# Unused tiles shift three operands of the matmuls against the weight tiles by multiples of 64 bytes

## The chip, the cores and the metric

The kernel runs on one core of a Trainium2 chip. The metric is the device time of one execution in microseconds (us); lower is better. TensorE (PE in the profile) multiplies, and a separate instruction loads its stationary operand (PEld). VectorE is DVE, ScalarE is ACT, GpSimd is POOL, SyncE is SP.

## What is computed

Two transformer blocks run one after the other on 256 tokens of width 2048, in float32. The first has four mixers (pooling, spatial gating, sliding-window attention, convolution), the second a state-space and an attention group, and then an expert layer with 16384 experts. Nearly all of the arithmetic is in products with large weight matrices:

```python
h = jnp.einsum('bsd,de->bse', x, w_in[l])                       # 2048 x 18688
merged = merged + gates[:, :, i] * jnp.einsum('bsc,cd->bsd', branches[i], w_branch[l, i])
out = jnp.einsum('bsd,de->bse', merged, w_out[l])
...
proj = h @ w_in                                                 # second block
x = x + jnp.concatenate([y_ssd, y_fox], axis=-1) @ w_out
q = (t @ wq)                                                    # expert layer: keys
act = jax.nn.gelu(jnp.einsum('thkd,td->thk', u[ib], tb))        # 16384 experts, u and v
return jnp.einsum('thk,thkd->td', gb * act, v[ib])
```

The kernel multiplies the tokens with all rows of `u` and all of `v`, and weights the results with a matrix that is zero for experts that were not chosen.

## The kernel before

**Weights come as a stream of chunks.** Each chunk is 128 partitions by 2048 float32. SyncE loads it into a tile `wr`; then `split` cuts it into halves of 1024 and makes two tiles of each: ScalarE rounds it to `wh` (float32r), and VectorE writes the rest, `wr - wh`, to `wl`. The activations are held in the same two parts: `XH` and `XL` (128 x 16 x 256), `YH` and `YL` (128 x 8 x 256) for the outputs of the four mixers, and `whh` and `whl` for the last product.

**Each product is three matmuls**: high by high, low by high, high by low. Four forms carry nearly all of the matmuls:

- `T_chunk`: 128 weight columns are stationary (`wh`, `wh`, `wl`), and 256 columns of `XH`, `XL`, `XH` move. All of `w_in`, most of the second block, `wq` and `u` go this way.
- `wb_chunk`: the same with `YH`, `YL`, `YH` moving, for `w_branch`.
- `N_chunk`: turned round, 128 columns of `XH`, `XL`, `XH` are stationary and 512 columns of `wh`, `wh`, `wl` move (`w_out`, and parts of both input products).
- `V_chunk`: as `N_chunk`, with `whh`, `whl`, `whh` stationary, for `v` (the last 700 us).

In a profile's row `pm<-XL,wh` the first name behind the arrow moves and the second is stationary; `pm` and `bg` are tiles of PSUM. Every matmul has a weight load of its own.

**Between the chunks**, background tasks (`bg()`, which calls `tasks.tick`) issue the small matmuls of the mixers and of the expert choice; the rows name them `bg<-...`. The order of all of them is made when the program is built, from a table of costs.

**Where tiles lie.** A pool lays its tiles one behind the other in a partition, in the order in which the code asks for them. The pool `per` has `XH`, `XL`, `X0`, `X1`, constants and small tiles; behind it come the pools of `wr`, `wh` and `wl`, then `a1` with `B4`, `gap`, `YH`, `YL`, `R`, `CV`, `GC`, `VQ` and small ones. `gap` is padding, of which 16 columns are used (`sk`). A block of `XH` or `YH` that moves is 1024 bytes long, and a stationary block of weights 512 bytes, and every block begins at a multiple of its length from its tile's start. So the distance of any moving block to any stationary block, modulo 512 bytes, is that of the tiles' starts.

Of the kernel before, what the change touches and what calls it, by code (L numbers as in the profile page):

```python
# [6 lines left out]
F32 = mybir.dt.float32  # L7
# [8 lines left out]
P = 128  # L16
# [181 lines left out]
def kern(tc, A, out):  # L198
    nc = tc.nc
    with ExitStack() as ctx:  # L200
        ctx.enter_context(tc.manual_schedule())
        _kern(tc, nc, ctx, A, out)


def _kern(tc, nc, ctx, A, out):
    tasks = Tasks(4)
    V, SC, G, PE = Meter(nc.vector, tasks, "dve"), Meter(nc.scalar, tasks, "act"), nc.gpsimd, Meter(nc.tensor, tasks, "pe")
    per = ctx.enter_context(tc.tile_pool(name="per", bufs=1))
# [4 lines left out]
    dram = ctx.enter_context(tc.tile_pool(name="dram", bufs=1, space=DRAM))  # L213

    XH = per.tile([P, KT, S], FR, name="XH")
    XL = per.tile([P, KT, S], FR, name="XL")
    X = [per.tile([P, D], F32, name=f"X{t}") for t in range(2)]
    cst = per.tile([P, 7, P], F32, name="cst")
    par = per.tile([P, N_PAR], F32, name="par")
# [13 lines left out]
    def pv(name, i=0, n=1):  # L233
        o, _ = PAR[name]
        return par[:, o + i:o + i + n]

    def row_ap(name):
        o, w = ROW[name]
        src = A["rows"]
        return bass.AP(tensor=src.tensor, offset=src.offset + o, ap=[[0, P], [1, w]])  # L240
# [51 lines left out]
    def T_chunk(evac):  # L292
        def fn(half, hi, lo):
# [5 lines left out]
            for kk in range(8):  # L299
                k = half * 8 + kk  # L300
                PE.matmul(o, h[:, kk], XH[:, k], start=k == 0, stop=False)
                PE.matmul(o, h[:, kk], XL[:, k], start=False, stop=False)
                PE.matmul(o, l[:, kk], XH[:, k], start=False, stop=k == KT - 1)
                if kk == 2:
# [5 lines left out]
    def N_chunk(kq, evac, korder=(0, 1, 2, 3), hold=False, lead=None):  # L310
        def fn(half, hi, lo):
# [6 lines left out]
            def part(t, kq, half, h, l):  # L318
                ts = slice(t * P, (t + 1) * P)
                for kk in range(2):  # L320
                    k = korder[kq] * 4 + half * 2 + kk
                    first = kq == 0 and half == 0 and kk == 0
                    last = kq == 3 and half == 1 and kk == 1
                    PE.matmul(ps[t], XH[:, k, ts], h[:, kk], start=first, stop=False)
                    PE.matmul(ps[t], XL[:, k, ts], h[:, kk], start=False, stop=False)
                    PE.matmul(ps[t], XH[:, k, ts], l[:, kk], start=False, stop=last)
                    if t == 0 and kk == 0:
# [44 lines left out]
    a1 = p1.enter_context(tc.tile_pool(name="a1", bufs=1))  # L372
    w1 = p1.enter_context(tc.tile_pool(name="w1", bufs=2))

    B4 = [a1.tile([P, 1024], F32, name=f"B4{i}") for i in range(4)]
    gap = a1.tile([P, 176], F32, name="gap")
    YH = a1.tile([P, 8, S], FR, name="YH")
    YL = a1.tile([P, 8, S], FR, name="YL")
    R = a1.tile([P, 8 * 286 + 8 * 272], F32, name="R")
    AP_ = R[:, :8 * 272].rearrange("p (j t) -> p j t", j=8)  # L380
# [6 lines left out]
    Q = VQ.rearrange("p (j t) -> p j t", j=8)  # L387
    U_ = X[0].rearrange("p (j t) -> p j t", j=8)
    GA = X[1].rearrange("p (j t) -> p j t", j=8)
    kT = a1.tile([P, S], F32, name="kT")  # L390
# [15 lines left out]
    def start_split():  # L406
        for g in range(4):
            SC.copy(XH[:, g * 4:(g + 1) * 4], xq[g])
            V.tensor_sub(XL[:, g * 4:(g + 1) * 4], xq[g], XH[:, g * 4:(g + 1) * 4].bitcast(F32))
            if g < 2:  # L410
# [87 lines left out]
    def conv_gen(ln):  # L498
# [13 lines left out]
        for stat in range(2):  # L512
# [4 lines left out]
            m = w1.tile([P, S], F32, name="cm")  # L517
            V.tensor_reduce(m, (sq if stat else CV).rearrange("p j t -> p t j"), axis=AX.X, op=OP.add)
            yield WAIT
# [102 lines left out]
    def attn_gen(u):  # L622
        def make(ln):
# [24 lines left out]
            m2 = sm[:, 0, :nq].rearrange("p (v j) -> p v j", v=2)  # L648
            V.tensor_reduce(sm[:, 0, :nq], L3, axis=AX.X, op=OP.max)
            V.tensor_tensor(m2, m2, sks, op=OP.max)  # L650
# [58 lines left out]
    def split_Y(src):  # L709
        for g in range(4):  # L710
            s = slice(2 * g, 2 * g + 2)
            SC.copy(YH[:, s], src[:, s])
            V.tensor_sub(YL[:, s], src[:, s], YH[:, s].bitcast(F32))

# [9 lines left out]
    def wb_chunk(br, jj):  # L724
        def fn(half, hi, lo):
# [3 lines left out]
            for k in range(8):  # L729
                PE.matmul(o, h[:, k], YH[:, k], start=k == 0, stop=False)  # L730
                PE.matmul(o, h[:, k], YL[:, k], start=False, stop=False)
                PE.matmul(o, l[:, k], YH[:, k], start=False, stop=k == 7)
                if k == 2:
# [21 lines left out]
    for br, (_, need, ysrc) in enumerate(order):  # L755
# [4 lines left out]
        for jj in range(8):  # L760
            def pre_y(need=need, ysrc=ysrc, br=br):
# [5 lines left out]
                if br == 2:  # L767
                    nc.gpsimd.dma_start(X[0], A["xN"][0])
                    nc.gpsimd.dma_start(X[1], A["xN"][1])
                    nc.gpsimd.dma_start(GC.rearrange("p j t -> p (j t)"), row_ap("ln_g"))  # L770
# [16 lines left out]
    def split_M(a, b):  # L787
        for g in range(a, b, 2):
            s = slice(g, g + 2)
            SC.copy(XH[:, s], M[:, s])  # L790
            V.tensor_sub(XL[:, s], M[:, s], XH[:, s].bitcast(F32))

# [28 lines left out]
    def to_T(t, lnw, hooks={}):  # L821
        for k0 in range(0, KT, 2):
# [6 lines left out]
            for k in (k0, k0 + 1):  # L829
                V.scalar_tensor_tensor(XL[:, k, t * P:(t + 1) * P], p[:, k - k0], pv(lnw, k),  # L830
                                       hs[:, k - k0].bitcast(F32), op0=OP.mult, op1=OP.subtract)
# [430 lines left out]
    def split_y(g0, g1):  # L1262
        YS, YF = b2["YS"], b2["YF"]
        for g in range(g0, g1, 2):
            s = slice(g, g + 2)
            y = YS[:, s] if g < 8 else YF[:, g - 8:g - 6]
            SC.copy(XH[:, s], y)
            V.tensor_sub(XL[:, s], y, XH[:, s].bitcast(F32))

# [498 lines left out]
```

## Time and profile before

| | |
|---|---|
| median of 3 runs | 3110.59 us (3110.5 to 3112.77) |
| the profiled execution | 3108.64 us, of it 3106.9 us from the first to the last instruction (the span) |
| PE busy | 3062.3 us, 99% of the span, 22026 matmuls |
| PE weight loads busy | 2858.2 us, 92% |
| DVE, ACT, POOL busy | 71%, 51%, 7% |
| granted TensorE clock | 0.995 of full speed over the span |

Matmuls are pipelined: one is shown for 276 to 281 ns, but in a row of them the next begins after a little over 113 ns. Busy time of PE therefore says only that there is always a matmul in flight. The number to read is the distance from one start to the next, the spacing. It comes from the start times of a timeline, or from a stretch's length divided by its count of matmuls; such a count includes those that reach over the stretch's edges, about two.

### The profile page before, as it was taken

The numbers are of one execution on the slowest core, as the hardware profiler recorded it, in microseconds if no ns is written. First come the engines' busy times: TensorE is split into PE (matmuls) and PEld (weight loads), VectorE is DVE, ScalarE is ACT, GpSimd is POOL, SyncE is SP. The second block draws the span as 40 slices with busy tenths as digits, with TensorE's granted clock in tenths as the row PEclk, the third lists the DMA queues.
The fourth block names the chain that finished last, engine by engine and source line by source line (L and its number), as shares of the span: only waits on it lengthen the run. The fifth ranks groups of instructions, "written<-read, shape, count | busy, mean of one in ns | idle before, by whom it ended". The sixth has DMA issues, their size and how long they took to land.

```text
span 3106.9 us, 53221 instructions
## 1 busy us (share of the span) xinstructions
PE 3062.3 (99%) x22026; PEld 2858.2 (92%) x22026; DVE 2200.2 (71%) x3173; ACT 1577.5 (51%) x2205; POOL 223.8 (7%) x187
## 2 busy tenths in 40 slices
PE   8999999999999989999999999999999999999998
PEld 8899999999999869897799999999999888888887
DVE  8899865555555567655579989788796666666665
ACT  4444565444444445555444457667675444444444
POOL 0000000000000020100000003232240000000000
PEclk9999999999999989999999999999999999999999
DMA  7555555555555535433545665766758766666664
GB/s 275 182 200 199 182 182 188 203 182 199 190 202 182 188 121 190 149 135 138 190 150 178 230 214 189 263 235 227 269 195 323 284 234 228 255 244 246 240 218 149
DMA packets 92226, 640.62 MB, mean 206 GB/s; under 512 B 10272, under 2 KB 10448, under 8 KB 17744
## 3 DMA queue, kind: packets, MB, share of 16 engines
q1 hardware_dynamic: 78192, 559.06, 50.2%
q0 software_dynamic: 13504, 77.63, 6.9%
q8 instruction: 173, 2.83, 0.4%
q14 instruction: 69, 0.57, 0.1%
q10 hardware_dynamic: 288, 0.52, 0.0%
HBM read 601.53 MB, written 35.65 MB: 205 GB/s over the span
## 4 chain that ended last, share of the span: by engine, by line
PE 97%; ACT 1%; DVE 1%; issue 1%; DMA 0%; SPq 0%; DVEq 0%; ACTq 0%
PE pm L194 92%; PE bg L194 4%; ACT wh L194 0%; DMA wr<-w_in 0%; DVE wl L194 0%; DVE X L194 0%; DVE XL L194 0%; ACT XH L194 0%; ACT KZ L194 0%; ACT L194 0%; SPq L398 0%; ACT PX L194 0%; ACT XS L194 0%; DVE PX L194 0%; DVE keys L194 0%
## 5 line engine op out<-in xcount | busy, mean ns | idle before, releaser
L194 DVE TENSOR_TENSOR wl<-wr,wh 128x1024 fp32r<-128x1024 f32 x1050 | 1291.3, 1233 | 833.6 <-ACT wh L194 824.3
L194 ACT CAST wh<-wr 128x1024 fp32r<-128x1024 f32 x1054 | 1109.0, 1053 | 1383.1 <-PE pm L194 1330.1
L194 PE MATMUL pm<-XH,wh 128*128 128x256 f32 x4976 | 1393.6, 280 | 8.0 <-ACT wh L194 8.0
L194 PE MATMUL pm<-XH,wl 128*128 128x256 f32 x4976 | 1383.3, 278 | 1.1 <-DVE wl L194 1.1
L194 PE MATMUL pm<-XL,wh 128*128 128x256 f32 x4976 | 1383.0, 278 | 0.0
L194 PEld LDWEIGHTS pm<-XH,wh 128*128 128x128 f32 x4976 | 940.5, 189 | 12.8 <-ACT wh L194 8.0
L194 PEld LDWEIGHTS pm<-XL,wh 128*128 128x128 f32 x4976 | 937.1, 188 | 1.8 <-issue 1.4
L194 PEld LDWEIGHTS pm<-XH,wl 128*128 128x128 f32 x4976 | 935.1, 188 | 1.6 <-DVE wl L194 1.6
L194 PE MATMUL pm<-wh,whl 128*128 128x512 f32 x1024 | 398.3, 389 | 0.0
L194 PE MATMUL pm<-wh,whh 128*128 128x512 f32 x1024 | 398.3, 389 | 0.0
L194 PE MATMUL pm<-wl,whh 128*128 128x512 f32 x1024 | 398.3, 389 | 0.0
L194 PEld LDWEIGHTS pm<-wh,whh 128*128 128x128 f32 x1024 | 192.2, 188 | 39.9
L194 PEld LDWEIGHTS pm<-wh,whl 128*128 128x128 f32 x1024 | 192.2, 188 | 39.9
L194 PEld LDWEIGHTS pm<-wl,whh 128*128 128x128 f32 x1024 | 192.2, 188 | 39.9
L194 PE MATMUL pm<-wh,XH 128*128 128x512 f32 x448 | 178.8, 399 | 1.8 <-ACT XH L194 1.8
L194 PE MATMUL pm<-wh,XL 128*128 128x512 f32 x448 | 176.9, 395 | 1.9 <-DVE XL L194 1.9
L194 PE MATMUL pm<-wl,XH 128*128 128x512 f32 x448 | 177.0, 395 | 0.0
L1453 POOL TENSOR_TENSOR keys<-cst,t 128x512 f32<-128x512 f32 x64 | 136.5, 2132 | 209.6 <-ACT ga L194 209.4
L194 PE MATMUL pm<-YH,wh 128*128 128x256 f32 x512 | 144.1, 281 | 0.0
L194 PE MATMUL pm<-YL,wh 128*128 128x256 f32 x512 | 143.7, 281 | 0.0
L194 PE MATMUL pm<-YH,wl 128*128 128x256 f32 x512 | 143.7, 281 | 0.0
L194 DVE SCALAR_TENSOR_TENSOR CV<-R,par,CV 128x256 f32<-128x256 f32 x240 | 116.8, 487 | 7.3
(276 smaller groups left out, 2381.8 us busy)
## 6 DMA issues: line engine op xcount, KB each, us to landing
wr<-w_in SPq DMA_DIRECT2D x190, 1024.0 KB, 4.8
wr<-uT SPq DMA_DIRECT2D x128, 1024.0 KB, 4.9
wr<-v SPq DMA_DIRECT2D x128, 1024.0 KB, 4.9
wr<-w_branch SPq DMA_DIRECT2D x32, 1024.0 KB, 4.8
wr<-w_out SPq DMA_DIRECT2D x32, 1024.0 KB, 4.8
wr<-wq SPq DMA_DIRECT2D x16, 1024.0 KB, 4.8
Ad<-ast POOLq DMA_DIRECT2D x16, 1024.0 KB, 5.1
Gd<-stg POOLq DMA_DIRECT2D x16, 1024.0 KB, 11.5
```

The source lines that it names most:

```text
L194: return f(out, *a, **k)
L1453: G.tensor_tensor(x, it, t3[:, 0, n0:n0 + 4, None].to_broadcast([P, 4, P]), op=OP.subtract)
```

## The change

Three tiles that nothing reads or writes are added, and `gap` is made 128 bytes shorter:

```diff
     XH = per.tile([P, KT, S], FR, name="XH")
+    per.tile([P, 16], F32, name="gaph")
     XL = per.tile([P, KT, S], FR, name="XL")
+    per.tile([P, 112], F32, name="gapx")
...
-    gap = a1.tile([P, 176], F32, name="gap")
+    gap = a1.tile([P, 144], F32, name="gap")
     YH = a1.tile([P, 8, S], FR, name="YH")
+    a1.tile([P, 16], F32, name="gapy")
     YL = a1.tile([P, 8, S], FR, name="YL")
```

`gaph` is 64 bytes and `gapx` 448, together 512; so all that lies behind them in `per`, and the weight tiles, keep their place modulo 512. On every engine the built program has the same instructions in the same order with the same waits as before. What differs is addresses:

| start in the partition, modulo 512 | before | after |
|---|---|---|
| `XH` | 128 | 128 |
| `XL` | 128 | 192 |
| `YH` | 128 | 0 |
| `YL` | 128 | 64 |
| `wh`, `wl` (all buffers), `whh`, `whl` | 448 | 448 |
| `R`; `CV`, `GC`, `VQ` | 128; 64 | 64; 0 |
| `ga`, `gb` (expert choice) | 0 | 0 |

The distance, start of the moving tile minus start of the stationary tile modulo 512, becomes:

| moving, stationary | matmuls | before | after |
|---|---|---|---|
| `XH`, `wh` and `XH`, `wl` | 2 x 4976 | 192 | 192 |
| `XL`, `wh` | 4976 | 192 | 256 |
| `YH`, `wh` and `YH`, `wl` | 2 x 512 | 192 | 64 |
| `YL`, `wh` | 512 | 192 | 128 |
| `wh`, `XH` and `wl`, `XH` | 2 x 448 | 320 | 320 |
| `wh`, `XL` | 448 | 320 | 256 |
| `wh` or `wl`, `whh` or `whl` | 3 x 1024 | 0 | 0 |
| `gb`, `ga` | 256 | 0 | 0 |

## Rows read from the trace of the kernel before

**Rows 1.** The page: busy by engine, granted clock in 40 slices, the chain.

```profile
PE 3062.3 (99%) x22026; PEld 2858.2 (92%) x22026; DVE 2200.2 (71%) x3173; ACT 1577.5 (51%) x2205; POOL 223.8 (7%) x187
...
PEclk9999999999999989999999999999999999999999
...
PE 97%; ACT 1%; DVE 1%; issue 1%; DMA 0%; SPq 0%; DVEq 0%; ACTq 0%
PE pm L194 92%; PE bg L194 4%; ACT wh L194 0%; DMA wr<-w_in 0%; DVE wl L194 0%; DVE X L194 0%; DVE XL L194 0%; ACT XH L194 0%; ACT KZ L194 0%; ACT L194 0%; SPq L398 0%; ACT PX L194 0%; ACT XS L194 0%; DVE PX L194 0%; DVE keys L194 0%
```

**Rows 2.** The page's groups, one per form: count | busy us, mean ns | idle before.

```profile
L194 PE MATMUL pm<-XL,wh 128*128 128x256 f32 x4976 | 1383.0, 278 | 0.0
...
L194 PE MATMUL pm<-wh,whl 128*128 128x512 f32 x1024 | 398.3, 389 | 0.0
...
L194 PE MATMUL pm<-wh,XL 128*128 128x512 f32 x448 | 176.9, 395 | 1.9 <-DVE XL L194 1.9
...
L194 PE MATMUL pm<-YL,wh 128*128 128x256 f32 x512 | 143.7, 281 | 0.0
```

**Rows 3.** Timeline of PE, two stretches of T_chunk: start us, us, what.

```profile
195.04 0.28 PE L194 MATMUL pm<-XH,wh 128*128 128x256 f32 x1
195.16 0.28 PE L194 MATMUL pm<-XL,wh 128*128 128x256 f32 x1
...
196.10 0.28 PE L194 MATMUL pm<-XH,wh 128*128 128x256 f32 x1
...
204.15 0.28 PE L194 MATMUL pm<-XH,wh 128*128 128x256 f32 x1
...
205.17 0.28 PE L194 MATMUL pm<-XH,wh 128*128 128x256 f32 x1
```

**Rows 4.** Timeline of the weight loads beside the second stretch.

```profile
204.15 0.19 PEld L194 LDWEIGHTS pm<-XL,wh 128*128 128x128 f32 x1
204.26 0.19 PEld L194 LDWEIGHTS pm<-XH,wl 128*128 128x128 f32 x1
```

**Rows 5.** Timeline of PE: background matmuls between two stretches.

```profile
198.81 0.28 PE L194 MATMUL pm<-XH,wl 128*128 128x256 f32 x1
198.93 0.60 PE L194 MATMUL bg<-B,VQ 128*128 128x128 f32 x4
199.29 0.37 PE L194 MATMUL pm<-XH,wh 128*128 128x256 f32 x1
...
510.86 0.66 PE L194 MATMUL bg<-B,vN 128*64 128x128 f32 x8
511.45 0.38 PE L194 MATMUL pm<-XH,wh 128*128 128x256 f32 x1
```

**Rows 6.** Windows, PE: stretch, busy (matmuls), granted clock, DMA share, GB/s.

```profile
514.00:1038.00 524.00, 524.00 (x4451) 1.00 0.54 192
1040.00:1126.00 86.00, 86.00 (x370) 1.00 0.53 184
1675.00:1855.00 180.00, 179.85 (x1587) 1.00 0.61 216
```

**Rows 7.** Windows of the tile XL, then of YL: the matmuls that read it.

```profile
190.00:513.00 323.00, 219.39 (x789) 1.00 0.54 189
514.00:1038.00 524.00, 287.74 (x1024) 1.00 0.54 192
1675.00:2402.00 727.00, 562.11 (x2036) 1.00 0.65 236
...
514.00:1038.00 524.00, 128.99 (x460) 1.00 0.54 192
```

**Rows 8.** Timeline of PE, first and last of long rows: N_chunk, then V_chunk.

```profile
100.14 0.39 PE L194 MATMUL pm<-wh,XH 128*128 128x512 f32 x1
...
141.34 0.39 PE L194 MATMUL pm<-wh,XH 128*128 128x512 f32 x1
...
2500.08 0.39 PE L194 MATMUL pm<-wh,whl 128*128 128x512 f32 x1
...
2539.97 0.39 PE L194 MATMUL pm<-wh,whh 128*128 128x512 f32 x1
```

**Rows 9.** Timeline of PE: a background group of the expert choice.

```profile
1858.56 0.28 PE L194 MATMUL pm<-XH,wl 128*128 128x256 f32 x1
1858.67 0.63 PE L194 MATMUL bg<-gb,ga 128*128 128x256 f32 x4
1859.15 0.28 PE L194 MATMUL pm<-XH,wh 128*128 128x256 f32 x1
1859.26 0.28 PE L194 MATMUL pm<-XL,wh 128*128 128x256 f32 x1
...
1860.17 0.28 PE L194 MATMUL pm<-XH,wh 128*128 128x256 f32 x1
```

## The prediction

> **What bounds the kernel now.** I read the page first: its chain of work lies on PE for 97% of the span, nearly all of it in the matmuls that write `pm`, and the granted clock stands at 0.9 or more of its upper level, 2.4 GHz, in 39 of 40 slices [rows 1]. Data, splits and evictions are hidden: in the groups the idle time ahead of the matmuls is 0.0 to 1.9 us over hundreds or thousands of them [rows 2]. So the time is the sum of the spacings of some 22,000 matmuls, and a change of addresses can only count through a spacing. No instruction, wait or transfer is added, removed or moved.
>
> The second view is the timeline of PE, and there one form, T_chunk, has two paces. From 195.04 to 196.10 us nine spacings take 1.06 us, 117.8 ns each; from 204.15 to 205.17 us nine take 1.02 us, 113.3 ns each [rows 3]. Operands, shapes and distances are the same, nothing waits, and the clock is the full one. I call them the wide and the tight pace; they differ by 4.4 ns a matmul. A pace holds until other matmuls come between: the group at 198.93 us stands between the wide stretch and the tight one, and the group at 510.86 us begins a wide stretch [rows 5] that then lasts, since no further group comes: 524 us from 514 us on hold 4451 matmuls, two of them over the edges, 117.8 ns each; N_chunk behind it keeps on, 86 us for 370, 233.5 ns. The expert layer has the tight one instead: 180 us for 1587, some 113.5 ns with its few small gaps [rows 6].
>
> So something that is neither a wait nor the clock lengthens the spacing. The weight load of the next matmul begins when the current one begins: `XH`, `wh` moves from 204.15 us on, and the load for `XL`, `wh` behind it starts at the same 204.15 us [rows 3, 4]. My reading, which the trace suggests and does not prove, is that the moving stream and the next weight load meet in SBUF, and that their relative place decides how often one holds the other up; the pace would come from the phase between the two, and the distance of the addresses would be the other half of the same sum.
>
> One pair of rows speaks of the distance alone. N_chunk and V_chunk have the same shape, 512 moving columns to one load; V_chunk runs at distance 0 and N_chunk at 320. In N_chunk, entered from a tight stretch, 180 spacings from 100.14 to 141.34 us take 41.20 us, 228.9 ns each; in V_chunk 176 spacings from 2500.08 to 2539.97 us take 39.89 us, 226.7 ns each [rows 8]. That is 2.2 ns a matmul between two distances.
>
> **The change part by part.** The sum is made against the profiled execution, 3108.64 us, which lies 1.95 us under the median of the three runs.
>
> *XL against wh in T_chunk, 192 to 256, 4976 matmuls [rows 2].* The trace has no row for 256 at this width. Bounds: at best XL loses what the wide pace costs it. Of the XL matmuls 1023 lie in the long wide stretch, and of the 788 from 190 to 513 us, where the groups of rows 5 alternate the paces, I take half (an estimate); with as rough a 200 in the other mixed places that is some 1600 [rows 7], so 1600 x 4.4 ns = -7 us. At worst 256 behaves as the worst that I see at 256 columns: in the expert choice `gb` moves over `ga` at distance 0, and six spacings around such a group, from 1858.56 to 1859.26 us, take 0.70 us, 116.7 ns each, 3.3 more than the tight 113.3 (the starts are rounded to 10 ns, so up to 4.5) [rows 9]; 4976 x 4.5 ns = +22 us. In between stands the pair of rows 8: if 256 is to 192 as 320 is to 0, it costs 2.2 ns, 4976 x 2.2 ns = +11 us. I take that, because 256 lies halfway between 192, whose tight pace is the least of any form here (half of V_chunk's 226.7 is also 113.3), and 320, which is the longer of the two in rows 8.
>
> *YH and YL, 192 to 64 and 128, 512 of each of three matmuls [rows 2].* 459 of the 512 triples lie in the long wide stretch [rows 7], where they pay 3 x 4.4 = 13.3 ns, 6 us together. Bounds: at best all of that vanishes, -6 us; at worst the 4.5 ns of rows 9 come on top of the wide pace that they have now, 1536 x 4.5 ns = +7 us. Neither 64 nor 128 has a row of its own, so I take 0.
>
> *XL as stationary in N_chunk, 320 to 256, 448 matmuls [rows 2].* Treating 256 as like 320, as above, this is 0; as like V_chunk's distance it is 448 x -2.2 ns = -1 us.
>
> *`R`, `CV`, `GC`, `VQ` and small tiles move by 64 bytes.* VectorE and ScalarE work on them, with 29% and 49% of the span free [rows 1]; nil, and a longer operation there would lie under PE's stream.
>
> *Which pace each stretch gets.* Taken as now.
>
> Sum: +11 us, 3108.6 to 3120, and as a median 3122 us, 0.4% slower.
>
> A rule speaks against any effect. The Trainium skill, "SBUF — State Buffer", "Who interferes with whom", says that TensorE has two independent read ports, one for the moving operand and one for the weight load, and that it never waits on anyone; "TensorE: Matmul & The Clock Gate", "Step-by-step: what each phase is for", says that loading the next weights takes no read bandwidth from the running matmul. By that rule the sum is 0 and the time 3111 us. The two paces of rows 3 at one clock, without a wait, do not agree with it, nor do the two of rows 8.
>
> **The rivals.**
>
> *The wide pace goes (faster).* The long wide stretch hangs on one group at 510.86 us. If the new distances shift the phase so that this group leaves the tight pace behind it, 4449 matmuls gain 4.4 ns, 19.8 us, and the 368 of N_chunk behind them 233.5 - 228.9 = 4.6 ns, 1.7 us. With XL at 0 to 2.2 ns the whole is -21 to -10 us: 3089 to 3100, say 3095 us. For it: the groups flip the pace between neighbouring stretches [rows 5], so which one a stretch gets hangs on a little shift. Against: the flips follow from the groups, which stay. It decides from the first stretch in which a different pace stands at the same matmul.
>
> *Nothing moves.* Distances of whole 64-byte steps might be alike as 192 and 0 are in their best pace, with N_chunk's 2.2 ns owed to its operands' layout and not the distance. Then 3111 us, give or take what a changed pace in a short stretch does, 3 us.
>
> *The tight stretches fall to the wide pace (much slower).* If XL's hold-up shifts the phase within each triple, the tight pace no longer sustains itself. The stretch from 1675 to 2402 us alone has 2035 triples [rows 7]: 6105 x 4.4 ns = 27 us, and XL's own 11 us come on top: 3149 us. For it: a tight pace is found only where all three matmuls of a triple have one distance. Against: after each `gb` group, at other distances, the tight pace is back [rows 9]: eight spacings from 1859.26 to 1860.17 us take 0.91 us, 113.8 ns each.
>
> That the change does not do what it says is excluded: the starts are read from the built program.
>
> **How the numbers follow.** About 0.2%, 6 us, is what a measurement of this kernel can tell from no change. The forecast, 3117 to 3133 us, has 0.42; it is the likeliest, and the predicted time is its 3122 us. The faster rival has 0.23, no change 0.20, the much slower one 0.15. Slower is 0.42 + 0.15 = 0.57. The range 3090 to 3152 us reaches from the better part of the faster rival to just over the much slower one's 3149 us; outside it I leave some 0.07 below (the Y gain on top of the faster rival) and 0.08 above (XL at 4.5 ns and the wide pace together).
>
> **What would show each step right or wrong.** In the expert layer from 1675 us on, where `XH` and `XL` alone move, three spacings take 340 ns now; my sum wants some 342, the much slower rival 353 or more, no change 340. The stretch from 514 us tells the pace by its count of matmuls: about 4451 in 524 us now, about 4620 if it turns tight. Y's price is read there from the triples of `YH`, `YL`, against those of `XH`, `XL` beside them: equal now. V_chunk must stay at 226.7 ns, as none of its operands moves; if it changes, the reading by distances is wrong. The prediction fails if 256 is as good as 192, or if the paces are dealt anew, which would outweigh all the terms.

## The result: slower by 1.4%

| | before | after |
|---|---|---|
| median | 3111.68 us (3110.5 to 3119.08, 4 runs) | 3155.8 us (3155.28 to 3158.05, 4 runs) |
| profiled execution | 3108.64 us, span 3106.9 us | 3156.3 us, span 3154.6 us |

The ratio is 1.0139, with a 95% interval from 1.0123 to 1.0155. The forecast was 3122 us with a range of 3090 to 3152 us: the sign was right, the size was not, and the time lies just outside the range.

The page of after, its lines that answer to [rows 1, 2]:

```profile
PE 3111.6 (99%) x22026; PEld 2909.9 (92%) x22026; DVE 2207.3 (70%) x3173; ACT 1577.1 (50%) x2205; POOL 198.6 (6%) x187
...
PEclk9999999999999989999999999999999999999999
...
PE 97%; ACT 1%; DVE 1%; issue 1%; DMA 0%; DVEq 0%; SPq 0%; ACTq 0%
...
L194 PE MATMUL pm<-XL,wh 128*128 128x256 f32 x4976 | 1402.2, 282 | 0.0
```

The same instructions run, on the same share of the chain, at the same granted clock, with the same idle time of 0.0 ahead of the matmuls. PE's busy time grew by 49.3 us, about as much as the span, 47.7 us, and that of its weight loads by 51.7 us; DVE's grew by 7.1 us, with the same 1% of the chain. So the loss is in spacings; the page can't say in which.

Windows of PE in after say where (stretch, busy (matmuls), granted clock, DMA share, GB/s); the first is the start of the first block, the second the long stretch of [rows 6], the third the expert layer:

```profile
20.00:98.00 78.00, 78.00 (x656) 1.00 0.64 230
514.00:1038.00 524.00, 524.00 (x4459) 1.00 0.55 191
1675.00:1855.00 180.00, 180.00 (x1515) 1.00 0.57 202
```

and the first of them in the kernel before, which [rows 6] does not have:

```profile
20.00:98.00 78.00, 78.00 (x691) 1.00 0.64 234
```

A count includes about two matmuls over the edges. The long stretch, wide before, is as it was: 4459 against 4451. What was tight is not: 78 us hold 656 matmuls instead of 691, 119.3 ns each instead of 113.2, and the expert layer 1515 instead of 1587, 119.0 instead of 113.5.

The timeline of PE in after gives the paces themselves: two stretches of T_chunk, a row of N_chunk, a row of V_chunk (start us, us, what), which answer to [rows 3, 8]:

```profile
604.88 0.28 PE L194 MATMUL pm<-XH,wh 128*128 128x256 f32 x1
...
607.00 0.28 PE L194 MATMUL pm<-XH,wh 128*128 128x256 f32 x1
```

```profile
1699.79 0.28 PE L194 MATMUL pm<-XH,wh 128*128 128x256 f32 x1
...
1702.30 0.28 PE L194 MATMUL pm<-XH,wh 128*128 128x256 f32 x1
```

```profile
1100.03 0.39 PE L194 MATMUL pm<-wl,XH 128*128 128x512 f32 x1
...
1114.46 0.39 PE L194 MATMUL pm<-wl,XH 128*128 128x512 f32 x1
...
2499.91 0.39 PE L194 MATMUL pm<-wh,whh 128*128 128x512 f32 x1
...
2539.35 0.39 PE L194 MATMUL pm<-wh,whh 128*128 128x512 f32 x1
```

Eighteen spacings from 604.88 us take 2.12 us, 117.8 ns each. Twenty-one from 1699.79 us take 2.51 us, 119.5 ns. N_chunk has 229.0 ns (63 spacings in 14.43 us), and V_chunk the 226.7 ns of before (174 in 39.44 us).

From the start times of all matmuls I took the length of every triple (three matmuls of one block, `XH`,`wh` to the next `XH`,`wh`) and averaged over six triples at a time:

| triple | before | after |
|---|---|---|
| X (`XH`,`wh`; `XL`,`wh`; `XH`,`wl`) | 340.0 ns in 65% of the blocks of six, 353.3 in 35% | 353.3 ns in 61%, 357.8 in 39%, 340 nowhere |
| Y (the same with `YH`, `YL`) | 353.3 | 353.3 or 352.5 |
| N_chunk | 686.7 or 700.0 | 686.7 |
| V_chunk | 680.0 | 680.0 |

Summed over the triples that have no gap in them, the time above 340 ns (680 in the turned forms) grew from 22.9 to 73.2 us for X, from 6.4 to 6.6 for Y, fell from 4.7 to 3.2 for N_chunk and stayed at 0 for V_chunk: +49.0 us, the whole growth of the busy time. The loss is X's alone.

It is not spread over X evenly. The order of the matmuls is the same in both kernels, so each triple can be set against itself. The 3095 X triples that were tight before (up to 346 ns, 340.1 on average) have 355.6 ns in after, +48.1 us; the 1604 that were wide have 353.9 instead of 353.3, +1.0 us. (These are the triples with the next one of the same kind right behind.)

The size hangs a little on the execution that was profiled. Three kernels below, e11, e12 and e14, have the distances of before and 27.3 to 29.7 us above 340 ns in X, where the profile of before has 22.9. Against them the loss in X is 44 to 46 us and not 50.

### The profile page after: what moved, and what is told of

It is laid out like the page before. It is cut to its first block, busy times and chain, and to the rows that moved or that the text cites. A ratio compares the mean times of both kernels' runs of the same rounds, so it can differ in the third digit from the quotient of the medians.

```text
span 3154.6 us, 53221 instructions
## 1 busy us (share of the span) xinstructions
PE 3111.6 (99%) x22026; PEld 2909.9 (92%) x22026; DVE 2207.3 (70%) x3173; ACT 1577.1 (50%) x2205; POOL 198.6 (6%) x187
## 4 chain that ended last, share of the span: by engine, by line
PE 97%; ACT 1%; DVE 1%; issue 1%; DMA 0%; DVEq 0%; SPq 0%; ACTq 0%
PE pm L194 93%; PE bg L194 4%; ACT wh L194 0%; DVE wl L194 0%; DVE X L194 0%; DVE XL L194 0%; DMA wr<-w_in 0%; ACT XH L194 0%; ACT KZ L194 0%; ACT L194 0%; ACT PX L194 0%; ACT XS L194 0%; DVE PX L194 0%; DVE keys L194 0%; ACT RB L194 0%
## 5 line engine op out<-in xcount | busy, mean ns | idle before, releaser
L194 PE MATMUL pm<-XH,wh 128*128 128x256 f32 x4976 | 1412.9, 284 | 8.0 <-ACT wh L194 8.0
L194 PE MATMUL pm<-XL,wh 128*128 128x256 f32 x4976 | 1402.2, 282 | 0.0
L1456 POOL TENSOR_TENSOR keys<-cst,t 128x512 f32<-128x512 f32 x64 | 111.3, 1738 | 239.6 <-ACT ga L194 239.4
```

Source lines behind the costliest of these rows:

```text
L194: return f(out, *a, **k)
L1456: G.tensor_tensor(x, it, t3[:, 0, n0:n0 + 4, None].to_broadcast([P, 4, P]), op=OP.subtract)
```

## The experiments

The runs share their comparison: the kernel before ran on the same chip each time, and its time is given behind the slash. It took 3109.8 to 3121.5 us over all of them, and all experiments but e11 and e13 have one execution, so a single time says nothing below some 10 us. The verdicts rest on the lengths of triples, which are the same to 0.1 ns wherever a pace stands. Which share of the triples has which pace is known for one execution of each kernel.

### Which of the moved tiles it is: e1, e2

e1 moves `XL` alone:

```diff
     XH = per.tile([P, KT, S], FR, name="XH")
+    per.tile([P, 16], F32, name="gaph")
     XL = per.tile([P, KT, S], FR, name="XL")
+    per.tile([P, 112], F32, name="gapx")
```

> Only XL moves by 64 bytes (distance 192 to 256); YH and YL keep 192. Theory A, a lengthened triple in T_chunk comes from XL alone: T_chunk triples of XH, XL as in the changed kernel, 353.3 or 357.8 ns instead of 340.0 or 353.3, and the time 3156 us give or take 5. Rival, the whole effect hangs on the pace that each stretch happens to get: triples of 340 ns are still to be found in some stretches, and the time lies anywhere from 3110 to 3156 us.

e2 moves `YH` and `YL` alone, to the distances that they have in after:

```diff
-    gap = a1.tile([P, 176], F32, name="gap")
+    gap = a1.tile([P, 16], F32, name="gap")
     YH = a1.tile([P, 8, S], FR, name="YH")
+    a1.tile([P, 16], F32, name="gapy")
     YL = a1.tile([P, 8, S], FR, name="YL")
+    a1.tile([P, 16], F32, name="gapr")
```

> Only YH and YL move (192 to 64 and 128); XH and XL keep 192. Theory A: the triples of XH and XL are 340.0 or 353.3 ns as before, those of YH and YL about 353 ns as in both kernels, and the time 3111 us give or take 5. Rival, Y's distances change the pace that the stretches of XH and XL between them get: the long stretch from 514 us turns to 340 ns, and the time is 3090 us, or the expert layer turns to 353 ns and it is 3138 us.

Measured: e1 3153.31 us / 3117.04; e2 3109.28 / 3117.04. Windows of PE, first of e1, then of e2:

```profile
20.00:98.00 78.00, 78.00 (x664) 1.00 0.65 235
600.00:1000.00 400.00, 400.00 (x3404) 1.00 0.56 195
1675.00:1855.00 180.00, 180.00 (x1514) 1.00 0.57 200
```

```profile
20.00:98.00 78.00, 78.00 (x665) 1.00 0.66 236
600.00:1000.00 400.00, 400.00 (x3486) 1.00 0.56 197
```

The X triples of e1 are those of after, 353.3 or 357.8 ns and never 340, and their time above 340 ns sums to 75.9 us (73.2 in after). So `XL` alone makes the whole loss. In the long stretch Y and X stand side by side and go different ways. Before, 400 us of it held 3399 matmuls, both wide:

```profile
600.00:1000.00 400.00, 400.00 (x3399) 1.00 0.55 192
```

In e1 Y, at its old distance, is tight; the timeline of PE in e1:

```profile
643.03 0.28 PE L194 MATMUL pm<-YH,wh 128*128 128x256 f32 x1
...
645.75 0.28 PE L194 MATMUL pm<-YH,wh 128*128 128x256 f32 x1
```

24 spacings in 2.72 us, 113.3 ns. In e2 it is the other way round: Y has 353.3 ns, and the X chunks between are back at 340, which is why 400 us hold 3486 matmuls instead of the 3399 of before. So a pace is not handed on from matmul to matmul regardless of its operands, as I had it: at a change of the distances it can change. The two moves do not simply add up: with `XL` moved, Y is tight at its old distance (e1, 0.6 us above 340 ns in all) and wide at its new ones (after, 6.6 us), while before it was wide at the old (6.4 us). Against before the term "Y: 0" is measured; against e1 the same move costs 6 us.

### Is it the distance, or the mixture: e3

Two readings were left. Either 256 is bad in itself (A1), or a triple suffers because its three distances differ (A2). e3 gives all three the distance 256:

```diff
+    per.tile([P, 16], F32, name="gap0")
     XH = per.tile([P, KT, S], FR, name="XH")
     XL = per.tile([P, KT, S], FR, name="XL")
+    per.tile([P, 112], F32, name="gapx")
```

> XH and XL both move by 64 bytes, so that all three matmuls of a T_chunk triple have distance 256. Theory A1, 256 is a bad distance by itself: no triple of 340 ns, all at 353 ns or more, time over 3140 us. Theory A2, it is the mixture of 192 and 256 within a triple that breaks the tight pace: triples of 340 or 353 ns are back, time 3090 to 3135 us by which pace the stretches get. N_chunk is at 256 in all three then (320 before).

Measured: 3170.98 us / 3117.04. The first window and one of N_chunk, PE in e3:

```profile
20.00:98.00 78.00, 78.00 (x652) 1.00 0.66 233
106.00:146.00 40.00, 40.00 (x178) 1.00 0.54 188
```

78 us for 650 matmuls is 120.0 ns, one pace everywhere, and worse than the mixture; A2 falls. N_chunk, whose stationary `XH` and `XL` are now both at 256, has 680.0 ns a triple, 226.7 a matmul: in the form with 512 moving columns 256 is the best distance, in that with 256 columns the worst. The two forms differ in more than the columns, since in N_chunk the weights move and the activations are stationary; which of the two turns the order round is not shown.

### Own load or next load: e4

The prediction blamed the load of the next matmul, which starts together with the current one [rows 4]. e4 shifts `XL` and `wl` both by 64 bytes. Then every moving block of X keeps the distance 192 to the weights that are loaded next, while to its own it has 192, 256 and 128:

```diff
+    per.tile([P, 16], F32, name="gaph")
     XL = per.tile([P, KT, S], FR, name="XL")
+    per.tile([P, 112], F32, name="gapx")
...
+        if hc == 0:
+            wspl.tile([P, 16], F32, name="gapw", bufs=1)
...
+        if hc == 0:
+            wspl.tile([P, 112], F32, name="gapv", bufs=1)
```

(`gapw` lies ahead of the tiles of `wl`, `gapv` behind them.)

> XL and all wl tiles move by 64 bytes. A matmul runs beside the weight load of the next one. Theory L, what counts is the distance of the moving block to the block that is loaded beside it: it is 192 for all three matmuls of a T_chunk triple again (XH beside wh, XL beside wl, XH beside wh), so triples of 340.0 and 353.3 ns as before; V_chunk gets 0, 0, 64 and may change. Rival O, what counts is the distance of a matmul's own two blocks: 192, 256, 128 in a triple, so no triple of 340 ns and the time over 3140 us.

Measured: 3179.72 us / 3117.04. The first window and the last 660 us, V_chunk, of PE in e4:

```profile
20.00:98.00 78.00, 78.00 (x660) 1.00 0.65 234
2480.00:3140.00 660.00, 660.00 (x2847) 1.00 0.64 230
```

The X triples have 355.6 ns and never 340, so the distance to the next load cannot be all that counts: theory L as I had put it falls. V_chunk, where `wl` now moves at 64 over `whh`, went from 226.7 to 232.0 ns (660 us for 2845), 16.4 us together. It had not changed in any other run. Which two streams meet stays open: the run excludes one pair as the only cause and proves no other.

e4 and e1 differ in nothing but the place of `wl`. `YH` and `YL` lie in both where they lay before, and yet Y's triples, 340.0 ns in most of e1 (341.2 on average), have 353.5 to 355.5 ns in e4 and are nowhere tight. So the address of the stationary tile counts too, and not that of the moving tile alone.

### The distance from 0 to 320: e5 to e10

Six kernels put `XH`, `XL`, `YH` and `YL` all at one distance; the paddings shift what lies behind them by 0 or 512 bytes, so nothing else moves modulo 512. e5, for distance 0, stands for all:

```diff
+    per.tile([P, 80], F32, name="gap0")
     XH = per.tile([P, KT, S], FR, name="XH")
     XL = per.tile([P, KT, S], FR, name="XL")
+    per.tile([P, 48], F32, name="gapx")
...
-    gap = a1.tile([P, 176], F32, name="gap")
+    gap = a1.tile([P, 128], F32, name="gap")
     YH = a1.tile([P, 8, S], FR, name="YH")
     YL = a1.tile([P, 8, S], FR, name="YL")
+    a1.tile([P, 48], F32, name="gapr")
```

> XH, XL, YH, YL all at distance 0 to the weights, so each form has one distance (T_chunk 0, N_chunk 0). The experiment with XH and XL at 256 gave one pace of 120.0 ns in T_chunk and 226.7 ns in N_chunk. Theory P, the odd multiples of 64 have the two paces and the even ones one pace of 120 ns: T_chunk 120 ns everywhere, N_chunk 226.7 ns like V_chunk at 0, time 3178 us give or take 8 (5488 triples at 20 ns over 340). Rival Q, only distances around 256 are bad: T_chunk at 113.3 to 117.8 ns, time 3075 to 3135 us.

> All four activation tiles at distance 64 in T_chunk (448 in N_chunk). Theory P (odd multiples of 64 have two paces): T_chunk 113.3 or 117.8 ns, N_chunk as with 320, 228.9 or 233.3 ns, time 3075 to 3135 us. Rival Q, the further from 256 the better: T_chunk at 113.3 ns everywhere, 3075 us.

> All four activation tiles at distance 128 in T_chunk (384 in N_chunk). Theory P (even multiples of 64 have one pace of 120 ns): T_chunk 120 ns, time 3178 us give or take 10. Rival Q (only distances around 256 are bad): 113.3 to 117.8 ns, time 3075 to 3135 us.

> All four activation tiles at distance 320 in T_chunk (192 in N_chunk). Theory P (odd multiples): T_chunk 113.3 or 117.8 ns, time 3075 to 3135 us. Rival Q (distances around 256 are bad, at both sides alike): T_chunk as at 192, 113.3 or 117.8 ns, the same. A third reading, that the price rises from 192 over 256 on to 320: T_chunk over 120 ns and over 3190 us. N_chunk at 192 tells whether 512 columns have at 192 what 256 columns have: 226.7 ns as the tight pace.

> All four activation tiles at distance 160 in T_chunk (352 in N_chunk): halfway between 128 (118.6 or 120 ns) and 192 (113.3 or 117.8 ns). Theory P64, what counts is which 64-byte piece the two streams are in, with a period of 128: halfway lies between the two, 115 to 119 ns, time 3110 to 3170 us. Rival, halfway belongs to neither and both paces are 113.3 ns: 3080 us.

> All four activation tiles at distance 224 in T_chunk (288 in N_chunk): halfway between 192 (113.3 or 117.8 ns) and 256 (120.0 ns). Theory P64, a period of 128 bytes: 115 to 119 ns, time 3110 to 3170 us, and much like 160. Rival, both paces are 113.3 ns: 3080 us.

The window of the start, PE, in e5 to e10 in this order:

```profile
20.00:98.00 78.00, 78.00 (x652) 1.00 0.64 234
```

```profile
20.00:98.00 78.00, 78.00 (x664) 1.00 0.65 235
```

```profile
20.00:98.00 78.00, 78.00 (x660) 1.00 0.64 233
```

```profile
20.00:98.00 78.00, 78.00 (x664) 1.00 0.64 233
```

```profile
20.00:98.00 78.00, 78.00 (x667) 1.00 0.64 233
```

```profile
20.00:98.00 78.00, 78.00 (x661) 1.00 0.64 234
```

With all triples, from the start times:

| run | distance, T_chunk | us / before | X triples, ns | distance, N_chunk | its triples |
|---|---|---|---|---|---|
| e5 | 0 | 3179.62 / 3117.09 | 360.0 | 0 | 680 |
| e6 | 64 | 3141.94 / 3117.09 | 340.0 in 21%, 353.3 in 79% | 448 | 700 |
| e7 | 128 | 3172.9 / 3117.09 | 355 to 357, 360.0 in 22% | 384 | 696 to 698 |
| e9 | 160 | 3161.33 / 3112.03 | 352 to 357 | 352 | 700 |
| before | 192 | | 340.0 in 65%, 353.3 in 35% | 320 | 687, 700 |
| e10 | 224 | 3161.54 / 3112.03 | 354.5 to 355.5 | 288 | 700 |
| e3 (X alone) | 256 | 3170.98 / 3117.04 | 360.0 | 256 | 680 |
| e8 | 320 | 3135.78 / 3117.09 | 340.0 in 29%, 353.3 in 71% | 192 | 700 |

What follows: the odd multiples of 64 bytes, 64, 192 and 320, have the same two paces, 113.3 and 117.8 ns; 0 and 256 have one, 120.0 ns; the halves between, 160 and 224, lie between and have no tight pace. Theory P, a period of 128 bytes, fails at 128 itself, where 360 ns is in 22% of the blocks and the others have 355 to 357 ns. A period of 256 bytes contradicts no row, 0 being like 256 and 64 like 320; no run tests it further. In N_chunk, with 512 moving columns, 0 and 256 are the best instead.

The table also shows why 64 and 320 lose 19 to 25 us to 192 although the paces of T_chunk are the same: the tight one is rarer there, and N_chunk has 700 ns throughout, each in the one execution profiled. Between two stretches of T_chunk the groups `keys,qp`, `B,VQ` and `mix,B` of the background flip the pace at 192 every time, as [rows 5] shows for `B,VQ`; at 64 and 320 they never do (16, 8 and 4 such places, wide on both sides). So in this 192 is not like 64 and 320, though a period of 128 would have them alike.

### Can the long wide stretch be turned: e11 to e14

The faster rival would have turned the stretch from 514 us. A small group of matmuls between the chunks was to do that by itself, in the kernel before, ahead of one chunk of `w_branch`. Its result is read by nobody. e11:

```diff
+            if br == 0 and jj == 3 and half in (0,):
+                z = pm.tile([P, 512], F32, name="pm")
+                for i in range(2):
+                    nc.tensor.matmul(z[:, i * P:(i + 1) * P], ident, tri, start=True, stop=True)
```

e12 sets `half in (0, 1)`: the group twice. The theory (F) was that any group between flips the pace.

> The kernel before, with all its distances, and one group of two float32 matmuls of 128 columns more, whose result nobody reads, ahead of the w_branch chunk at about 513 us. Theory F, a pace is a phase that such a group flips and that nothing else touches until the next group: the long stretch from 513 us on runs at 113.3 instead of 117.8 ns and N_chunk behind it at 228.9 instead of 233.3, -19.8 and -1.7 us, and the group costs some 0.6 us: 3090 us against 3111. Rival, the pace comes from something else in this stretch (the product with w_branch, what VectorE and ScalarE do there): it stays at 117.8 ns, 3111 us.

> As the experiment with one group, and a second equal group half a chunk (eight triples) later. Theory F: the first group flips the pace of eight triples to 113.3 ns, the second flips it back to 117.8 ns for the rest of the long stretch: 3112 us. Rival, the first group's gain had another reason (the shifted rotation of PSUM tiles, a later start): the stretch stays at 113.3 ns, 3090 us.

Measured: e11 3114.39 us (11 runs) / 3114.96 (15 runs), ratio 1.0 with an interval from 0.9991 to 1.0009; e12 3117.65 / 3114.96. The timeline of PE in e11 at the group, then a window:

```profile
517.11 0.61 PE L731 MATMUL pm<-cst 128*128 128x128 f32 x4
517.91 0.28 PE L194 MATMUL pm<-YH,wh 128*128 128x256 f32 x1
...
519.68 0.28 PE L194 MATMUL pm<-YH,wh 128*128 128x256 f32 x1
```

```profile
20.00:98.00 78.00, 78.00 (x664) 1.00 0.66 235
600.00:1000.00 400.00, 400.00 (x3399) 1.00 0.55 194
```

Behind the group 15 spacings take 1.77 us, 118.0 ns: the pace stays wide. F as stated falls; e12, built on it, is inconclusive. The first window shows something else: it lies ahead of the group, where the code is that of before, and yet it holds 664 matmuls, as many as the wide pace has, and not the 691 of before. So the pace that a stretch begins with is not settled by the code up to there. That it differs between executions of one and the same kernel is likely but not shown, since each kernel has one trace; I take it for part of the spread of the kernel before.

The second attempt takes a group whose operands lie in `B4`, the tile from which the flipping groups of [rows 5] read (F2: it is the group's addresses that count). e13 has it once, e14 twice:

```diff
-                    nc.tensor.matmul(z[:, i * P:(i + 1) * P], ident, tri, start=True, stop=True)
+                    nc.tensor.matmul(z[:, i * P:(i + 1) * P], B4[0][:, :P], B4[0][:, P:2 * P], start=True, stop=True)
```

> As the experiment with one more group of two float32 matmuls ahead of the w_branch chunk at about 513 us, but with both operands of the group in the tile B4, which starts at 448 modulo 512 as the weights do (they were constants at 128, and the pace did not change). In the kernel before, the groups with an operand at 448 (keys, B) flip the pace of T_chunk every time: 16 of 16 groups on keys, 8 of 8 on B with VQ. Theory F2, the addresses of the group decide whether it flips: the stretch from 513 us on runs at 113.3 ns, and the time is 3092 us against 3114. Rival, a group with this shape here cannot flip it, whatever its addresses: 117.8 ns and 3114 us.

> As the experiment with one group on B4, and a second equal group half a chunk (eight triples) later. Theory F2: tight for eight triples, then 117.8 ns again up to N_chunk, 3114 us. Rival, if the first group does change the pace but for the time that it takes rather than by a flip: tight or wide for the rest whichever the second group happens to leave.

Measured: e13 3095.44 us (3091.48 to 3101.23, 6 runs) / 3118.49 (11 runs), ratio 0.993 with an interval from 0.9916 to 0.9943; e14 3118.04 / 3118.49. The timeline of PE in e13, then windows:

```profile
513.05 0.28 PE L194 MATMUL pm<-XH,wl 128*128 128x256 f32 x1
513.17 0.60 PE L731 MATMUL pm<-B 128*128 128x128 f32 x4
...
513.97 0.28 PE L194 MATMUL pm<-YH,wh 128*128 128x256 f32 x1
...
515.00 0.28 PE L194 MATMUL pm<-YH,wh 128*128 128x256 f32 x1
```

```profile
600.00:1000.00 400.00, 400.00 (x3532) 1.00 0.57 200
1675.00:1855.00 180.00, 179.46 (x1527) 1.00 0.59 206
```

and the timeline of PE in e14, where the second group follows 3.2 us later:

```profile
518.12 0.60 PE L731 MATMUL pm<-B 128*128 128x128 f32 x4
...
518.92 0.28 PE L194 MATMUL pm<-YH,wh 128*128 128x256 f32 x1
...
520.96 0.28 PE L194 MATMUL pm<-YH,wh 128*128 128x256 f32 x1
...
521.30 0.60 PE L731 MATMUL pm<-B 128*128 128x128 f32 x4
...
522.10 0.28 PE L194 MATMUL pm<-YH,wh 128*128 128x256 f32 x1
...
522.46 0.28 PE L194 MATMUL pm<-YH,wh 128*128 128x256 f32 x1
```

In e13 nine spacings behind the group take 1.03 us, 114.4 ns with the starts' rounding to 10 ns, and the pace holds: 400 us have 3532 matmuls, 113.3 ns each, instead of 3399. In e14 the first group gives 18 spacings in 2.04 us, 113.3 ns, and the second takes it back: the next three take 0.36 us, and 600 to 1000 us hold 3398, as in before:

```profile
600.00:1000.00 400.00, 400.00 (x3398) 1.00 0.55 195
```

Both came out as F2 wanted, and e13 is faster than both kernels. What F2 adds to F, that it is the group's addresses, rests on two groups at one place; the tile that they read differs in its contents too, and no run keeps one and changes the other. Nor does every group that reads `B` flip: in the trace of before `B`,`vN` leaves a tight stretch tight at 436.66 us and makes one wide at 510.86 us [rows 5].

It is no full gain: in the profiled execution of e13 the expert layer began wide, 1527 matmuls in 180 us instead of 1587. Whether the added group has a part in that is not shown, for the pace of that layer varies without it: e12 and e14 both hold 3398 matmuls from 600 to 1000 us, and yet in the expert layer the one is wide and the other tight; PE in e12, then in e14:

```profile
1675.00:1855.00 180.00, 180.00 (x1531) 1.00 0.58 205
```

```profile
1675.00:1855.00 180.00, 180.00 (x1588) 1.00 0.60 211
```

## Why the prediction was wrong

**What bounds the kernel: right.** Spacings, not waits, clock or transfers. By the Trainium skill's rule that the ports are independent and TensorE waits on no one ("SBUF — State Buffer", "Who interferes with whom") the addresses would count for nothing. The traces do not agree: the same instructions at a granted clock of 1.00 have 120.0 ns in e5 and 113.3 in the tight stretches of before. Whether ports meet, or something else lengthens the spacing, no run shows.

**The step that failed is the term of `XL` at 256, +11 us: 2.2 ns on one matmul in three, in every stretch alike, with the paces of the stretches taken as now.** It measured some 50 us, and nearly all of it in triples that had been tight, on all three matmuls: 13.3 ns a triple where it became 353.3 and 17.8 where it became 357.8. Where the triple had been wide it cost next to nothing, 0.6 ns. Two errors make that up.

- *The matmul itself.* In the pace of 353.3 ns its three spacings are 117.1, 120.0 and 116.2 ns (`XH`,`wh`; `XL`,`wh`; `XH`,`wl`; means over all such blocks). `XL`'s 120.0 is what all three have in e3, 6.7 ns over the tight 113.3, where the bound was 4.5. It is no price that `XL` pays everywhere: in the wide pace of before the three have 118.1, 117.7 and 117.5 ns, so there the other two gave back what `XL` took, and in the pace of 357.8 `XL` has 118.9. The analogy "256 is to 192 as 320 is to 0" was wrong twice: 256 belongs to 0 and 320 to 192 (e5, e3, e8), and rows of 512 columns, from which I took it [rows 8], have the opposite order. The nearest row in form was [rows 9], 256 columns at distance 0. I used it only as the bound, and it mixed four matmuls of the group with the T_chunk matmuls around it; 116.7 was the mean of unlike things (117.8 from the starts before rounding), and the upper bound from it was too low. Inside the group, from the second start on, the spacings average 119.8 ns over all 64 such groups of the trace before, close to the 120.0 of e3 and e5.
- *The other two.* With `XL` at 256 no triple keeps the tight pace: the neighbours go from 113.3 to 116 to 121 ns. That was the mechanism of the "much slower" rival, to which I gave 0.15. Its row for it, that a tight pace is found only where a triple has one distance, was the better reading. Its row against, [rows 9], showed that the pace comes back after a group at other distances (behind 62 of the 64, and not behind each, as I wrote), which is not the same as living with one inside every triple. Its 3149 us is 6.8 us short of the 3155.8, and that it is so near is partly luck: it counted the 2035 tight triples of the expert layer alone, and those of the first block, 691 matmuls in the window from 20 us and now 656, fell with them; against that it added 11 us for `XL` in all stretches. The combination that I left outside the range, 4.5 ns on `XL` and the wide pace together, comes by my own terms to 22 + 27 = 49 us and is nearest, for the same mixed reasons.

In the sum: a mean X triple went from 344.6 ns (65% at 340, 35% at 353.3) to 355.1 (61% at 353.3, 39% at 357.8). 10.5 ns on 4976 triples is 52 us; the term was to be 11.

**YH and YL: right in the sum, not in the reason.** Y has 353.3 ns before and 353.3 or 352.5 after, and 353.3 in e2. But I took 0 because no row priced 64 or 128, and what the runs show, in one execution each, are two effects that happen to cancel: with `XL` moved alone Y is tight (e1), and with its own new distances as well it is wide again (after). The bound below, that the wide pace could go, was real: Y is tight in e1 and e13.

**N_chunk: right.** It gained 1.5 us in the profiled executions, where 1 us was the bound, but that is the share of 700 ns triples, 20 of 60 blocks before and none after, and not the new distance: e12, at the distances of before, has no 700 either, and 3.0 us above 680 against the 3.2 of after. The common triple has 686.7 ns in both. (The 233.5 ns of [rows 6] is 86 us for 368, which makes 233.7; the triples of 700 ns say 233.3.)

**`R`, `CV`, `GC`, `VQ`, V_chunk: right.** V_chunk stays at 226.7 ns, the mark named for the reading by distances.

**"Which pace each stretch gets: as now": wrong for X.** There is no 340 left to get, and this is the part of the failed step that made the loss. The faster rival did not happen in after (4459 against 4451 in the long stretch), but e13 shows its size to be real: 400 us hold 133 matmuls more (117.8 ns against 113.3), which on the 4449 of the stretch is 20 us, and the ratio is 0.993.

**The reading of the cause** (moving stream against the next load) is refuted in its pure form by e4. That the start addresses decide is shown by e1, e3 and e5 to e10, where nothing else changes, and by e4 against e1 that the stationary tile's counts as well as the moving one's. That only the distance between the two counts was not tested: no run shifts both alike. Why a pace persists, and what sets it, is open.

## What to carry to other kernels

Where a matrix engine's chain has no waits and a full clock, read spacings from start times, form by form and triple by triple; the busy share (99% in both kernels) and mean durations (278 and 282 ns, 1.4% apart) hide spacings that differ by 6%, 113.3 and 120.0 ns. Start addresses of moving and stationary tiles are then a parameter like a tile's size, to be measured for each form of matmul apart, and all operands of a sequence have to be at a good distance: here one in three at a bad one took the good pace from the other two. So price such an operand by what the whole sequence loses, and only where it has something to lose. One profile shows one deal of the paces; compare kernels by the paces that are possible in them and not by the shares alone. Price an unseen value by the row nearest in form, even if only one poor row has it, and don't carry an order over from another shape.

## What the runs showed of the hardware

- With 256 moving columns the spacing is 113.3 or 117.8 ns at 64, 192 and 320 bytes, 120.0 ns at 0 and 256, and has no tight pace at 128, 160 and 224 (before, e3, e5 to e10). With 512 columns, where the weights move, it is 226.7 ns at 0 and 256 and up to 233.3 at 192, 288, 320, 352 and 448.
- A pace holds over thousands of matmuls, 3532 in the 400 us of e13, and is flipped by four short matmul records of a group that takes 0.6 us, or not, by which tile that group reads (e11, e13, e14).
- One operand in three at 256 leaves no tight triple (after, e1); it costs 15.5 ns a triple where the pace was tight and 0.6 where it was wide.
- The pace at the start is not settled by the code. e13 and e14 have the same code and addresses up to 513 us and ran on the same chip; windows of PE, first e13, then e14, differ by 26 matmuls in 78 us:

```profile
20.00:98.00 78.00, 78.00 (x690) 1.00 0.64 234
```

```profile
20.00:98.00 78.00, 78.00 (x664) 1.00 0.65 232
```
